# A decoder trunk's second norm: spreading the token factors through DRAM instead of with a diagonal product

## The chip, the cores and the metric

The kernel runs on one core of one Trainium2 chip. The metric is the device time of one execution in microseconds (us). The engines are named as the profile names them: PE is TensorE (PEld its weight loads), DVE is VectorE, ACT is ScalarE, POOL is GpSimd and SP is SyncE, which here only issues the weight transfers.

## The reference

Two layers, each a gated linear recurrence and a sliding-window attention merged, and then a feed-forward block. 256 tokens, width 1024, hidden width 2816, float32. What matters here is the second norm of a layer and what follows it:

```python
def rmsnorm(x, g):
    xf = x.astype(jnp.float32)
    y = xf * lax.rsqrt(jnp.mean(xf * xf, axis=-1, keepdims=True) + EPS)
    return (y * g.astype(jnp.float32)).astype(x.dtype)
...
        x = x + mix @ w_o[l]

        h2 = rmsnorm(x, norm2[l])
        x = x + (jax.nn.silu(h2 @ w_gate[l]) * (h2 @ w_up[l])) @ w_down[l]
```

The norm multiplies each token's row by one factor, the inverse root of its mean square. A factor per token can be applied after the product with a weight matrix as well as before it.

## The kernel before

**Numbers.** Every float32 operand of a large product is cut in a high part, rounded to PE's fast float32 form, and a low part, the rest. ACT casts the high part of a weight (`wh<-raw`), DVE subtracts to get the low one (`wl<-raw,wh`). A product is then three PE products: high by high, high by low, low by high. In the form used for the gate and up products of the feed-forward block, `form_b`, the activations' two parts lie side by side as 512 columns, so that eight wide matmuls (128x512, with `wh`) and eight narrow ones (128x256, with `wl`) make one result of 128 hidden features by 256 tokens. ACT and DVE together drain it from PSUM: ACT copies one half (`COPY zg<-pg`), DVE adds the other (`zg<-pg,zg`); this pair is the function `join`, and DVE's addition is the last that reads the PSUM bank.

**The norm.** The class `Norm` transposes the activations by PE, multiplies by the gain, and cuts them in two parts (`xx`) without the token factors. The factors come out of sums of squares: ACT squares and sums, DVE adds, POOL raises to the power -1/2. That gives `r`, one column of 128 factors (one per partition) for each of the two tiles of 128 tokens. Where a result has tokens on the partitions, `r` is applied as a factor per partition. Where it has tokens along the free axis, as the gate sums do, the 256 factors are needed on all 128 partitions: that is `rb`, and two methods of the class make it. `spread` multiplies the identity by `r` on DVE (`dg`), multiplies a matrix of ones by this diagonal on PE (`rp`, a float32 product) and copies it to `rb` on ACT. `spread_by_row` transposes the two columns on PE to one row in PSUM (`row`), copies it to SBUF on DVE (`flat`), writes it to DRAM by a transfer issued by POOL (L410), and reads it back to all 128 partitions by a second one (L411). The first norm of each layer uses `spread_by_row`, with its result needed some 20 us later; the second norm uses `spread`.

**The feed-forward block.** `layer` works through groups of up to four blocks of 128 hidden features, two blocks at a time in `gate_up`. Such a pair of blocks, called a block below, has two gate sums `pg` and two up sums `pu`. In a layer's first block the order on PE is written out: half of the first `pg`, half of the first `pu`, their second halves (so that the last transposes of the norm fit between), then the call `spread2()`, then the second `pg`, and the second `pu`. After both gate sums are drained to `z`, the function `mid` multiplies `z` by `rb`, takes the sigmoid (`sgm`, on ACT) and multiplies again; the up sums are drained into the same tile `sgm` after that. The up sums get no factor, since that is applied per token after the down product.

**Buffers.** PSUM tiles with the tag `mm` rotate through four banks; a block takes all four (two `pg`, then two `pu`), and the next block the same four in the same order. The prepared weights have five buffers of each kind (`wh`, `wl`), and raw weights three (1 MB each), so weights are prepared up to about four units ahead. One unit is what one `pg` or `pu` needs.

**What sets the order.** PE's instructions stand in the order of the program. For the other engines a scheduler places instructions when the program is built, by its own estimates of when operands are ready; each engine then executes its list strictly in order. A few instructions are pinned with `tc.keep_in_program_order`, among them the two products with the identity and the two transposes of `r`. SP issues the loads of raw weights when a raw buffer has been read for the last time.

Of the kernel before, what the change touches and what calls it, by code (L numbers as in the profile page):

```python
# [44 lines left out]
def trunk(ctx, tc, x, norm1, w_in, lb_logits, hg_norm, attn_sinks, w_pa, w_pb, w_o, norm2,  # L45
# [32 lines left out]
    def psum(name, tag="mm"):  # L78
        return pp.tile([P, 512], F32, tag=tag, name=name, bufs=4 if tag == "mm" else 2)
# [356 lines left out]
    def finish(side):  # L436
        while side[0] is not None:
            step(side)
# [8 lines left out]
    def layer(l, n1):  # L447
# [461 lines left out]
        n2 = Norm(g2[:, l], f"n2_{l}")  # L909
# [21 lines left out]

        for p_ in parts:
            finish(p_)
        rs2, rb2, spread2 = n2.r, n2.wide(), n2.spread
        acc = [[psum(f"acc{l}{t}{c}", "at" if t == 0 else "hg") for c in range(2)] for t in range(NT)]

        def gate_up(gi, b, ah, al):
# [184 lines left out]
    for l in range(DEPTH):  # L1122
        hold = []

        def whole():
            hold.append((yield from layer(l, nx)))

        run(whole())
        nx = hold[0]
# [53 lines left out]
```

## Time and profile before

| | |
|---|---|
| Time, median of 3 runs | 929.61 us (929.11 to 930.15) |
| The profiled execution's own time | 929.29 us |
| Its span, first to last instruction | 927.5 us |
| PE busy | 919.1 us, 99% of the span |
| DVE busy | 675.0 us, 73% |
| ACT busy | 541.2 us, 58% |
| POOL busy | 19.5 us, 2% |
| Moved by DMA | 161.40 MB, 174 GB/s on average |

A row of the order of time reads: start in us, duration in us, engine, line of the program, operation, what is written and read with its shape, a count where neighbours are merged, and in brackets the idle time before it on its engine with what ended it. Almost all computing instructions stand at L59, a helper, so rows are told apart by the names of their tiles. For a matmul the duration contains a tail that overlaps the next one; its real cost is the distance to the next start.

### The profile page before, as it was taken

How to read it: one execution, taken by the hardware profiler on the slowest of the kernel's cores; microseconds unless marked ns; L12 is line 12 of the kernel's file. 1: busy time of each engine (PE TensorE's matmuls, PEld its weight loads, DVE VectorE, ACT ScalarE, POOL GpSimd, SP SyncE). 2: the span in 40 equal slices, each digit the busy share in tenths (PEclk: the TensorE clock that was granted, in tenths of full speed). 3: DMA queues.
4: the chain of work that ended last, by engine and by line, in shares of the span. 5: the costliest groups of instructions: out<-in, count | busy, mean ns of one | idle time of the engine just before them, and what ended most of it. 6: DMA issues, size and time to landing. Idle time of an engine off the chain costs nothing.

```text
span 927.5 us, 14425 instructions
## 1 busy us (share of the span) xinstructions
PE 919.1 (99%) x5716; PEld 780.6 (84%) x5716; DVE 675.0 (73%) x1175; ACT 541.2 (58%) x924; POOL 19.5 (2%) x31
## 2 busy tenths in 40 slices
PE   9999999999999999999999999999999999999997
PEld 7888888888888888888888888888888888888885
DVE  6678899656678766766866787996576787667765
ACT  7567964555456545545555779546463565545553
POOL 2000000001000000000000000000010000000000
PEclk9999999999999999999999999999999999999999
DMA  8725544644546555555555245466445555556641
GB/s 301 262 92 182 163 132 162 213 152 137 182 136 217 192 182 184 190 200 198 167 196 187 94 135 182 140 209 199 137 158 182 177 186 182 183 192 202 194 137 46
DMA packets 111395, 161.40 MB, mean 174 GB/s; under 512 B 2912, under 2 KB 64672, under 8 KB 111328
## 3 DMA queue, kind: packets, MB, share of 16 engines
q1 hardware_dynamic: 110848, 159.42, 52.4%
q8 instruction: 45, 0.74, 0.3%
q10 hardware_dynamic: 320, 0.79, 0.3%
q0 software_dynamic: 160, 0.26, 0.1%
q14 instruction: 22, 0.18, 0.1%
HBM read 159.42 MB, written 1.05 MB: 173 GB/s over the span
## 4 chain that ended last, share of the span: by engine, by line
PE 99%; DVE 0%; ACT 0%; issue 0%; POOL 0%; DVEq 0%; ACTq 0%; POOLq 0%
PE pg L59 13%; PE pu L59 13%; PE acc L59 13%; PE pb L59 10%; PE yb L59 5%; PE v L59 5%; PE gb L59 5%; PE wo L59 5%; PE gate L59 5%; PE ga L59 5%; PE ya L59 5%; PE aq L59 5%; PE akv L59 3%; PE qk L59 1%; PE pv L59 1%; PE o L59 1%
## 5 line engine op out<-in xcount | busy, mean ns | idle before, releaser
L59 DVE TENSOR_TENSOR wl<-raw,wh 128x1024 fp32r<-128x1024 f32 (+1 forms) x301 | 365.4, 1219 | 147.8 <-ACT wh L59 146.8
L59 ACT CAST wh<-raw 128x1024 fp32r<-128x1024 f32 (+1 forms) x301 | 315.1, 1052 | 173.6 <-PE acc L59 45.7
L59 PE MATMUL pu<-xx_n,wh 128*128 128x512 f32 x352 | 92.5, 393 | 0.0
L59 PE MATMUL pg<-xx_n,wh 128*128 128x512 f32 x352 | 92.0, 392 | 0.0
L59 PEld LDWEIGHTS pg<-xx_n,wh 128*128 128x128 f32 x352 | 63.1, 189 | 11.0
L59 PEld LDWEIGHTS pu<-xx_n,wh 128*128 128x128 f32 x352 | 63.0, 189 | 11.0
L59 PE MATMUL acc<-wh,ah 128*128 128x512 f32 x174 | 68.0, 391 | 0.0
L59 PE MATMUL acc<-wh,al 128*128 128x512 f32 x174 | 67.7, 389 | 0.0
L59 PE MATMUL acc<-wl,ah 128*128 128x512 f32 x174 | 67.7, 389 | 0.0
L59 PE MATMUL pb<-xx_n,wh 128*128 128x512 f32 x256 | 65.6, 394 | 0.0
L59 PEld LDWEIGHTS pb<-xx_n,wh 128*128 128x128 f32 x256 | 45.6, 189 | 8.6 <-issue 0.7
L59 PEld LDWEIGHTS pg<-xx_n,wl 128*128 128x128 f32 x352 | 48.4, 190 | 4.1 <-ACT xx_n L59 0.6
L59 PEld LDWEIGHTS pu<-xx_n,wl 128*128 128x128 f32 x352 | 48.4, 190 | 3.6
L59 PE MATMUL pg<-xx_n,wl 128*128 128x256 f32 x352 | 50.3, 284 | 0.0
L59 PE MATMUL pu<-xx_n,wl 128*128 128x256 f32 x352 | 49.7, 282 | 0.0
L59 ACT COPY zg<-pg 128x256 f32<-128x256 f32 x44 | 16.4, 372 | 53.4 <-PE pg L59 53.4
L59 PE MATMUL ga<-wh,xx_n 128*128 128x512 f32 x128 | 41.3, 394 | 0.0
L59 PE MATMUL v<-wh,xx_n 128*128 128x512 f32 x128 | 41.1, 395 | 0.0
L59 PE MATMUL gb<-wh,xx_n 128*128 128x512 f32 x128 | 40.7, 391 | 0.0
L59 PE MATMUL aq<-wh,xx_n 128*128 128x512 f32 x128 | 40.3, 391 | 0.0
L59 PE MATMUL gate<-wh,xx_n 128*128 128x512 f32 x128 | 40.3, 391 | 0.0
L59 PEld LDWEIGHTS acc<-wh,al 128*128 128x128 f32 x174 | 32.7, 188 | 6.8
(265 smaller groups left out, 1660.8 us busy)
## 6 DMA issues: line engine op xcount, KB each, us to landing
raw<-in_w_in SPq DMA_DIRECT2D x58, 1024.0 KB, 5.2
raw<-in_w_gate SPq DMA_DIRECT2D x22, 1024.0 KB, 5.1
raw<-in_w_up SPq DMA_DIRECT2D x22, 1024.0 KB, 5.1
raw<-in_w_down SPq DMA_DIRECT2D x22, 1024.0 KB, 5.0
raw<-in_w_pb SPq DMA_DIRECT2D x8, 1024.0 KB, 5.1
raw<-in_w_pa SPq DMA_DIRECT2D x8, 1024.0 KB, 5.0
raw<-in_w_o SPq DMA_DIRECT2D x8, 1024.0 KB, 5.0
raw<-in_w_in SPq DMA_DIRECT2D x3, 512.0 KB, 7.3
```

The costliest lines, as they stand in the source:

```text
L59: ins = call(*args, **kw)
```

## The change

In `layer`, the second norm's factors are spread by `spread_by_row` instead of `spread`. The call stands at the same place of the program, after the halves of the first gate and the first up sum:

```diff
         for p_ in parts:
             finish(p_)
-        rs2, rb2, spread2 = n2.r, n2.wide(), n2.spread
+        rs2, rb2, spread2 = n2.r, n2.wide(), n2.spread_by_row
         acc = [[psum(f"acc{l}{t}{c}", "at" if t == 0 else "hg") for c in range(2)] for t in range(NT)]
```

The two methods, both there before:

```python
        def spread(self):
            rp = psum(f"rp_{self.name}", "at")
            dg = sm.tile([P, S], F32, tag="dg", name=f"dg_{self.name}", bufs=1)
            for t in range(NT):
                tc.keep_in_program_order(V.tensor_scalar(dg[:, t * P:(t + 1) * P], ident, self.r[t], None, ALU.mult))
            T.matmul(rp[:, :S], ones, dg, start=True, stop=True)
            A.copy(self.rb[:, 0, :], rp[:, :S])

        def spread_by_row(self):
            row = dp.tile([NT, P], F32, tag=f"row_{self.name}", name=f"row_{self.name}")
            flat = sm.tile([1, S], F32, tag="flat", name=f"flat_{self.name}", bufs=1)
            ps = psum(f"row_{self.name}", "at")
            for t in range(NT):
                tc.keep_in_program_order(T.transpose(ps[0:1, t * P:(t + 1) * P], self.r[t], ident))
            V.tensor_copy(flat, ps[0:1, :S])
            nc.gpsimd.dma_start(row.rearrange("t (o p) -> o (t p)", o=1), flat)
            nc.gpsimd.dma_start(self.rb[:, 0, :], row.rearrange("t p -> (t p)").partition_broadcast(P))
```

On PE, in the first block of layer 0 (`pg_2855` is the block's second gate sum, `pu_2856` and `pu_2857` its up sums):

```order
 L59 MATMUL pu_2856<-xx_n_0_2635,wl_2819 128x256 x2
 L59 MATMUL pu_2856<-xx_n_0_2635,wh_2818 128x512 x4
-L59 MATMUL pg_2855<-xx_n_0_2635,wl_2809 128x256 x2
-L59 MATMUL rp_n_0_2894<-dg_n_0_2895,ones 128x256
-L59 MATMUL pg_2855<-xx_n_0_2635,wl_2809 128x256 x6
+L59 MATMUL row_n_0_2896<-ident,r_n_00_2638 1x128
+L59 MATMUL row_n_0_2896<-ident,r_n_01_2639 1x128
+L59 MATMUL pg_2855<-xx_n_0_2635,wl_2809 128x256 x8
 L59 MATMUL pg_2855<-xx_n_0_2635,wh_2808 128x512 x4
 L59 MATMUL pu_2857<-xx_n_0_2635,wh_2830 128x512 x4
```

The ones-by-diagonal product is gone from among the narrow matmuls, and the two transposes stand ahead of them. All else on PE keeps its order.

The same place on DVE before, from the first gate sum's drain to the drains of the first block's two up sums:

```order
L59 TENSOR_TENSOR zg_2858<-pg_2854,zg_2858 128x256
L59 TENSOR_SCALAR dg_n_0_2895<-ident,r_n_00_2638 128x128
L59 TENSOR_SCALAR dg_n_0_2895<-ident,r_n_01_2639 128x128
L59 TENSOR_TENSOR wl_2930<-raw_2806,wh_2929 128x1024
L59 TENSOR_TENSOR wl_2952<-raw_2828,wh_2951 128x1024
L59 TENSOR_TENSOR zg_2858<-pg_2855,zg_2858 128x256
L59 TENSOR_TENSOR zg_2858<-zg_2858,rb_n_0_2636 128x512
L59 TENSOR_TENSOR wl_2958<-raw_2828,wh_2957 128x1024
L59 TENSOR_TENSOR zg_2858<-zg_2858,sgm_2859 128x512
L59 TENSOR_TENSOR wl_2989<-raw_2927,wh_2988 128x1024
L59 TENSOR_TENSOR sgm_2859<-pu_2856,sgm_2859 128x256
L59 TENSOR_TENSOR sgm_2859<-pu_2857,sgm_2859 128x256
```

And now, from the weight split ahead of the copy on (`pg_2966` and `pg_2967` are the second block's gate sums, which were `pg_2964` and `pg_2965` before; weights made after this place have numbers higher by two):

```order
L59 TENSOR_TENSOR wl_2932<-raw_2806,wh_2931 128x1024
L59 COPY flat_n_0_2895<-row_n_0_2896 1x256
L59 TENSOR_TENSOR wl_2954<-raw_2828,wh_2953 128x1024
L59 TENSOR_TENSOR zg_2858<-pg_2855,zg_2858 128x256
L59 TENSOR_TENSOR wl_2960<-raw_2828,wh_2959 128x1024
L59 TENSOR_TENSOR wl_2991<-raw_2929,wh_2990 128x1024
L59 TENSOR_TENSOR zg_2858<-zg_2858,rb_n_0_2636 128x512
L59 TENSOR_TENSOR wl_3015<-raw_2929,wh_3014 128x1024
L59 TENSOR_TENSOR zg_2858<-zg_2858,sgm_2859 128x512
L59 TENSOR_TENSOR zg_2970<-pg_2966,zg_2970 128x256
L59 TENSOR_TENSOR zg_2970<-pg_2967,zg_2970 128x256
L59 TENSOR_TENSOR sgm_2859<-pu_2856,sgm_2859 128x256
```

The products with the identity are gone. The copy to `flat` stands behind one weight split; the product with `rb` stands two splits later than before; and the drains of the second block's gate sums, which stood behind those of the first block's up sums, now stand ahead of them.

On ACT, the rows from the drain of the first block's second gate sum on, now:

```order
L59 COPY zg_2858<-pg_2855 128x256
L59 CAST wh_2959<-raw_2828 128x1024
L59 CAST wh_2990<-raw_2929 128x1024
L59 CAST wh_3014<-raw_2929 128x1024
L59 ACTIVATE sgm_2859<-zg_2858 128x512
L59 COPY zg_2970<-pg_2966 128x256
L59 COPY zg_2970<-pg_2967 128x256
L59 COPY sgm_2859<-pu_2856 128x256
L59 COPY sgm_2859<-pu_2857 128x256
```

Before, the copy of `rp` to `rb` stood at their head, the sigmoid directly behind the first of these casts, and the copies of the up sums ahead of those of the second block's gate sums. From the end of the second block on the lists of all engines are the same again. POOL has two more transfers per layer, after the powers that make `r`. Layer 1 changes in the same way.

## The prediction

> **What bounds the kernel now.** I read the page first, then PE's waits, then the order of time around the two places of the change.
>
> ```profile
> span 927.5 us, 14425 instructions
> PE 919.1 (99%) x5716; PEld 780.6 (84%) x5716; DVE 675.0 (73%) x1175; ACT 541.2 (58%) x924; POOL 19.5 (2%) x31
> ...
> PEclk9999999999999999999999999999999999999999
> ...
> PE 99%; DVE 0%; ACT 0%; issue 0%; POOL 0%; DVEq 0%; ACTq 0%; POOLq 0%
> ```
>
> The chain that ended last is PE alone. The view of PE's waits has a single row:
>
> ```profile
> PE warm L59 <- POOL ident L59: 1.6, 1, 1.6
> ```
>
> So after its start PE never waits for another engine, and its granted clock stays full. What PE no longer executes shortens the run; any wait put in front of a PE instruction lengthens it, because no later PE gap exists that could absorb it. Idle time of DVE (73% busy) and ACT (58%) costs nothing until PE needs something from them.
>
> **The change part by part: PE's own work.** Removed per layer: the product of the ones matrix with the diagonal matrix, at this place (in order of time, layer 0):
>
> ```profile
> 286.75 0.40 PE L59 MATMUL pg<-xx_n,wl 128*128 128x256 f32 x2
> 287.07 0.70 PE L59 MATMUL rp_n<-dg_n,ones 128*128 128x256 f32 x2
> 287.42 1.06 PE L59 MATMUL pg<-xx_n,wl 128*128 128x256 f32 x6
> 288.32 1.09 PE L59 MATMUL pg<-xx_n,wh 128*128 128x512 f32 x4
> 290.16 1.12 PE L59 MATMUL pu<-xx_n,wl 128*128 128x256 f32 x8
> 291.11 1.09 PE L59 MATMUL pu<-xx_n,wh 128*128 128x512 f32 x4
> ```
>
> Eight narrow matmuls alone take 291.11 - 290.16 = 0.95 us; eight with the product among them take 288.32 - 286.75 = 1.57. The product costs 0.62. Added: two transposes of a 128x1 column, which the first norm already has:
>
> ```profile
> 27.15 0.39 PE L59 MATMUL aq<-wl,xx_n 128*128 128x512 f32 x1
> 27.38 0.40 PE L59 MATMUL aq<-wh,xx_n 128*128 128x512 f32 x1
> ...
> 28.05 0.38 PE L59 MATMUL row_n<-ident,r_n 128*1 128x128 f32 x2
> 28.19 0.48 PE L59 MATMUL aq<-wh,xx_n 128*128 128x512 f32 x1
> ...
> 28.50 0.39 PE L59 MATMUL aq<-wl,xx_n 128*128 128x512 f32 x1
> ```
>
> From the first transpose to the second aq after it are 0.45 us, of which one aq takes 0.23 (27.15 to 27.38): the pair costs 0.22. PE gains 0.62 - 0.22 = 0.40 per layer, and from there runs 0.4 ahead of the old times. DVE's two products with ident and ACT's copy of rp go too; they are off the path and worth nothing by themselves.
>
> **The new chain: when the row has come back.** DVE's copy to flat now stands behind a weight split, not at the place of the diagonal. The two executions of the same chain in the first norm price the rest; the second block of rows is of layer 1, and the last two are the broadcast's landing in each:
>
> ```profile
> 28.47 0.41 DVE L59 COPY flat_n<-row_n 1x256 f32<-1x256 f32 x1 [0.34 <-PE row_n L59]
> 29.18 0.71 POOL L410 DMA_DIRECT2D row_n<-flat_n  x1 [10.01 <-DVE flat_n L59]
> 31.98 0.57 POOL L411 DMA_DIRECT2D rb_n<-row_n  x1 [2.08 <-DMA row_n<-flat_n]
> ...
> 485.55 0.41 DVE L59 COPY flat_n<-row_n 1x256 f32<-1x256 f32 x1 [1.07 <-PE row_n L59]
> 486.25 0.57 POOL L410 DMA_DIRECT2D row_n<-flat_n  x1 [17.02 <-DVE flat_n L59]
> 488.44 0.56 POOL L411 DMA_DIRECT2D rb_n<-row_n  x1 [1.62 <-ACT aq L59]
> ...
> DMA to landing us min/median/max: 3.5/3.5/3.5
> ...
> DMA to landing us min/median/max: 4.3/4.3/4.3
> ```
>
> From the end of the copy to the first issue pass 0.30 and 0.29 us, between the issues 2.80 and 2.19, from the second issue to its landing 3.5 and 4.3: 6.6 and 6.8 in all. On POOL nothing else is queued then. Now the engines around the old place:
>
> ```profile
> 286.06 2.00 ACT L59 CAST wh<-raw 128x1024 fp32r<-128x1024 f32 x2
> 287.15 2.36 DVE L59 TENSOR_TENSOR wl<-raw,wh 128x1024 fp32r<-128x1024 f32 x2
> 290.31 0.69 DVE L59 TENSOR_TENSOR zg<-zg,rb_n 128x512 f32<-128x512 f32 x1
> 290.92 1.22 DVE L59 TENSOR_TENSOR wl<-raw,wh 128x1024 fp32r<-128x1024 f32 x1
> 292.29 1.05 ACT L59 CAST wh<-raw 128x1024 fp32r<-128x1024 f32 x1 [0.61 <-PE pu L59]
> 293.91 2.00 PE L59 MATMUL pg<-xx_n,wh 128*128 128x512 f32 x8
> 294.51 0.75 DVE L59 TENSOR_TENSOR sgm<-pu,sgm 128x256 f32<-128x256 f32 x2
> 295.04 0.37 ACT L59 COPY zg<-pg 128x256 f32<-128x256 f32 x1 [1.16 <-PE pg L59]
> 295.30 1.06 ACT L59 CAST wh<-raw 128x1024 fp32r<-128x1024 f32 x1
> 297.63 1.07 PE L59 MATMUL pu<-xx_n,wh 128*128 128x512 f32 x4
> 297.83 0.37 ACT L59 COPY zg<-pg 128x256 f32<-128x256 f32 x1 [0.95 <-PE pg L59]
> ```
>
> The split that now precedes the copy still waits for its cast (ACT, from 286.06), so it starts at 287.15 and leaves DVE at about 288.3 (of two splits in 2.36 us, the second starts 2.36 - 1.22 = 1.14 after the first). Copy 288.3 to 288.7, plus 6.6 to 6.8: the broadcast lands at 295.3 to 295.5. I add 0.2 for the wake of DVE (an estimate: in the first norm POOL issued 0.30 after the landing of its own row) and take **T = 295.6** for the product of zg with rb, which in the old run started at 290.31.
>
> **What is queued behind it.** By the new order DVE then executes, strictly one after the other: zg by rb, one weight split, zg by its sigmoid, two drains of the second block's gate sums (pg), and only then the drains of the first block's up sums (pu). In the old order the pu drains came at 294.51. Pitches from the rows: zg by rb 0.61 (290.31 to 290.92), the split 1.14, zg by sigmoid 0.61 (the same shape), the pg drains 0.33 each (two drains take 0.75, one 0.42), the pu drain 0.42: 3.44 us. The first pu bank is drained at 295.6 + 3.44 = 299.04. ACT's copies ahead of the drains fit between: the sigmoid ends near 297.0, the copies of both pg by 297.9 (the second follows the end of its PE product, 297.83 - 0.4), and that of pu follows zg by sigmoid.
>
> Who waits? The pool for these sums has four banks. Block one holds pg, pg, pu, pu; the second block's two pg take the first two, and its first pu has to take a pu bank. PE reaches this matmul at 297.63 - 0.40 = 297.23 and has to wait until about 299.1. **Stall 1.9 us per layer**, against the 0.4 gained: 1.5 net.
>
> Behind the stall nothing else is late: the splits of the next four weight units stand ahead of the drains, a unit lasts PE 2.8 us (eight wide matmuls at 0.23, eight narrow in 0.95), and the first split behind the drains is for a product that PE reaches four units, some 11 us, after the stall. Weight loads on SP hang on splits that stand ahead of zg by rb, or are needed far later; no cost. Both layers are alike: the old rows stand 456.9 us apart,
>
> ```profile
> L59 ACT COPY rb_n<-rp_n x2: 373/373/373, 288.0 to 744.9; 128x256 f32<-128x256 f32 x2
> ```
>
> so the sum is 2 x (1.9 - 0.4) = **+3.0 us**. The profiled execution took 929.29 us (span 927.5 and 1.8 around it): 932.3. The median of the runs is 929.61, 0.3 more, so it gives 932.6; I say 932.5.
>
> **Bounds.** Below: however early the row lands, the split behind zg by rb needs a cast of ACT which needs the weight buffer of the second block's first product. That product ended just ahead of 295.04, now 294.64; plus 1.06 the cast is ready at 295.7, and split to pu drain are 1.14 + 0.61 + 0.66 + 0.42 = 2.83: 298.5. The stall has a floor of 1.3, net 0.9 per layer, 931.4 in all. Above: a landing 1.4 us later (somewhat under twice the 0.8 between 3.5 and 4.3) makes T = 297.0, a stall of 3.3, net 2.9, 935.4.
>
> The Trainium skill ("DMA: Bandwidth & Descriptors", Anatomy of one DMA, the gpsimd path) gives each such transfer a fixed cost of about 2.0 us plus bytes over 436 GB/s, thus an estimate of 2.0 and 2.3 for the two; by that T would be near 293.6, the floor would hold, and the time would be 931.4. This trace's second transfer disagrees with 3.5 and 4.3, and I go by the trace.
>
> **The rivals.**
>
> *Hidden.* The drains come in time and only PE's 0.4 per layer is left: 929.6 - 0.8 = 928.8. For it: the old pu drains ended at 295.3, 2.4 us before PE needed the bank, and PE had no wait. It decides if DVE drains the first pu by 297.2, hence T at 293.8 or earlier and the cast of 295.30 off DVE's way. Against it: the measured chain gives 295.6, and the cast alone gives 298.5.
>
> *The row comes late.* The raw weight loads share the DMA engines with the broadcast; with a load on them at full rate the landing may exceed 4.3. Each further microsecond is one per layer; at T = 297 the time is 935.4. For it: 3.5 and 4.3 already differ by 0.8 for the same bytes. Against it: both were taken amid the same loads.
>
> *The clock drops too.* PE without work may lose speed when it restarts. The run's start bears on it:
>
> ```profile
> 6.48 0.79 PE L59 MATMUL akv<-wl,xx_n 128*128 128x512 f32 x1
> ...
> 8.99 0.39 PE L59 MATMUL akv<-wl,xx_n 128*128 128x512 f32 x1
> ```
>
> The same matmul took 0.79 us about 5 us after PE's first work and 0.39 later, half speed for 5 us or so, though the clock row shows full. If a stall set PE back to that, 5 us at half speed lose 2.5 per layer: 932.6 + 5.0 = 937.6 from the forecast, 940 with the late row. For it: PE would be idle for 1.9 to 3.3 us. Against it: at the start PE had done nothing at all, and here 1.9 us of idleness is preceded by 280 us of work. The Trainium skill ("TensorE: Matmul & The Clock Gate", Why this matters for your kernels) warns of gaps of more than about 3 us, after which the clock falls to half. By that the forecast's stall stays under it, and only the late row's reaches it; no wait of this trace shows which.
>
> **How the numbers follow.** Forecast, stall of 1.3 to 2.6 per layer: 0.67. Hidden: 0.10. Late row at full clock: 0.12. Clock drop: 0.11. The predicted time is the forecast's. 80% range: from 930.4, which leaves most of the hidden case out, to 936.0, which takes in the late row and leaves out most of the clock's. This kernel's measurement tells about 0.2% (1.9 us) from no change. Faster by more needs 1.9 us, more than the 1.24 of removed product work: 0.03. Within: nearly all of the hidden case and the forecast's floor, which lies just on the border: 0.17. Slower: 0.80.
>
> **What would show it.** In the new profile PE's waits get a row of pu waiting for DVE's sgm, twice, 1.9 us each; the rb product starts some 5 us later than before, near 295.6 and 752.5; DVE has an idle row released by the DMA of rb; the first pu of the second block starts near 299.1; part 2 keeps PEclk at 9. The row pair should cost PE 0.22. If PE has no new wait, the drain argument is wrong. If PE waits but the rb product starts near 294, the chain's price is wrong and ACT's cast is the floor. If the matmuls after the stall take twice their time, the clock case holds.

## The result, and the profile after

The changed kernel takes **937.95 us** (median of 4 runs, 936.77 to 938.92) against 929.88 for the kernel before on the same chip. The ratio is 1.0087 (95% interval 1.0075 to 1.0099): 8 us slower, where +3 was forecast, and above the range's upper end of 936.0. The profiled execution of the changed kernel took 938.92 us.

The page of the changed kernel, its span, PE's busy time, the clock in 40 slices and the engines of the chain that ended last:

```profile
span 936.9 us, 14440 instructions
...
PE 922.3 (98%) x5716; PEld 782.7 (84%) x5716; DVE 674.0 (72%) x1173; ACT 541.6 (58%) x922; POOL 21.8 (2%) x35
...
PEclk9999999999999999999999999999999989999999
...
PE 96%; DMA 2%; DVE 1%; issue 1%; ACT 0%; POOL 0%; DVEq 0%; ACTq 0%; POOLq 0%
```

The chain is no longer PE alone: DMA and DVE have 3% of it. PE is busy for 3.2 us more than before although it has less to do, and in one slice its clock isn't full. The view of PE's waits:

```profile
PE pu L59 <- DVE zg L59: 6.2, 2, 3.2
```

One new wait in each layer, 6.2 us in both together. Here is layer 0 in order of time:

```profile
287.33 0.38 PE L59 MATMUL row_n<-ident,r_n 128*1 128x128 f32 x2
...
288.50 1.09 PE L59 MATMUL pg<-xx_n,wh 128*128 128x512 f32 x4
288.87 0.40 DVE L59 COPY flat_n<-row_n 1x256 f32<-1x256 f32 x1
288.98 0.37 SPq L190 DMA_DIRECT2D raw<-in_w_up  x1
...
289.56 0.57 POOL L410 DMA_DIRECT2D row_n<-flat_n  x1 [5.15 <-DVE flat_n L59]
...
294.78 0.56 POOL L411 DMA_DIRECT2D rb_n<-row_n  x1 [4.65 <-DMA row_n<-flat_n]
...
298.17 0.69 DVE L59 TENSOR_TENSOR zg<-zg,rb_n 128x512 f32<-128x512 f32 x1 [3.40 <-DMA rb_n<-row_n]
...
300.52 0.75 DVE L59 TENSOR_TENSOR zg<-pg,zg 128x256 f32<-128x256 f32 x2
...
300.99 1.21 PE L59 MATMUL pu<-xx_n,wh 128*128 128x512 f32 x4 [3.01 <-DVE zg L59]
...
301.18 0.75 DVE L59 TENSOR_TENSOR sgm<-pu,sgm 128x256 f32<-128x256 f32 x2
...
302.04 1.11 PE L59 MATMUL pu<-xx_n,wl 128*128 128x256 f32 x8
```

Between the two POOL issues lie 5.22 us. The view of the DMA issues between 284 and 300 us has the KB of each and the us from issue to landing:

```profile
raw<-in_w_up SPq DMA_DIRECT2D x1, 1024.0 KB, 5.1
...
rb_n<-row_n POOLq DMA_DIRECT2D x1, 128.0 KB, 3.3
row_n<-flat_n POOLq DMA_DIRECT2D x1, 1.0 KB, 4.7
```

The 1 KB of the row needed 4.7 us. Then the broadcast takes 3.4 until DVE goes on, and 2.82 later PE has its bank: 3.01 us of waiting. (This execution is 0.58 us late here already, from its start; PE's row that began at 285.83 before begins at 286.41.) In layer 1 the same happens, and something more:

```profile
758.25 0.69 DVE L59 TENSOR_TENSOR zg<-zg,rb_n 128x512 f32<-128x512 f32 x1 [3.57 <-DMA rb_n<-row_n]
...
761.07 2.07 PE L59 MATMUL pu<-xx_n,wh 128*128 128x512 f32 x4 [3.19 <-DVE zg L59]
...
762.95 1.91 PE L59 MATMUL pu<-xx_n,wl 128*128 128x256 f32 x8
```

The four wide matmuls take 2.07 us where layer 0 has 1.21, the eight narrow ones 1.91 where it has 1.11. The stretches of time around it give the cause, the granted clock, third number from the end of each row:

```profile
758.00:760.00 2.00, 0.00 (x0) 0.00 (x0) 1.75 (x3) 1.02 (x3) 0.00 (x0) 1.00 0.00 0
760.00:761.00 1.00, 0.00 (x0) 0.00 (x0) 1.00 (x4) 0.43 (x3) 0.00 (x0) 0.67 0.00 0
761.00:763.00 2.00, 1.93 (x5) 1.54 (x6) 2.00 (x6) 1.67 (x4) 0.00 (x0) 0.50 0.75 215
763.00:765.00 2.00, 2.00 (x10) 1.98 (x9) 2.00 (x4) 0.86 (x2) 0.00 (x0) 0.50 0.87 310
...
767.00:769.00 2.00, 2.00 (x13) 1.79 (x13) 1.32 (x2) 0.92 (x2) 0.00 (x0) 0.96 0.00 0
```

From the wait's last part to shortly after 767 PE runs at half speed (the row left out has 0.50 too), which costs 6 x 0.5 + 2 x 0.04 = 3.1 us. In layer 0 the clock stays full after a wait of almost the same length.

The account of this execution goes against the profiled one of before, whose span is 9.4 us shorter (927.5). At the two waits PE's next product starts 3.18 and 3.36 us later than it would have: from start to start are 4.11 us (296.88 to 300.99) and 4.29 (756.78 to 761.07), where before the same distance is 0.93 (296.70 to 297.63). The view's 3.01 and 3.19 are shorter because they begin behind the tail of the product ahead. So: delays at the waits +6.5, removed work -0.8, clock +3.1, lateness from the start +0.6, together 9.4.

### The profile page after: what moved, and what is told of

Its sections match the earlier page's. It is cut to its first block, busy times and chain, and to the rows that moved or that the text cites. A ratio compares the mean times of both kernels' runs of the same rounds, so it can differ in the third digit from the quotient of the medians.

```text
span 936.9 us, 14440 instructions
## 1 busy us (share of the span) xinstructions
PE 922.3 (98%) x5716; PEld 782.7 (84%) x5716; DVE 674.0 (72%) x1173; ACT 541.6 (58%) x922; POOL 21.8 (2%) x35
## 3 DMA queue, kind: packets, MB, share of 16 engines
HBM read 159.68 MB, written 1.05 MB: 172 GB/s over the span
## 4 chain that ended last, share of the span: by engine, by line
PE 96%; DMA 2%; DVE 1%; issue 1%; ACT 0%; POOL 0%; DVEq 0%; ACTq 0%; POOLq 0%
PE pu L59 13%; PE acc L59 13%; PE pg L59 12%; PE pb L59 10%; PE yb L59 5%; PE v L59 5%; PE wo L59 5%; PE gb L59 5%; PE gate L59 5%; PE ga L59 5%; PE ya L59 5%; PE aq L59 5%; PE akv L59 3%; PE qk L59 1%; PE pv L59 1%; PE o L59 1%
## 5 line engine op out<-in xcount | busy, mean ns | idle before, releaser
L59 PE MATMUL pu<-xx_n,wh 128*128 128x512 f32 x352 | 94.9, 400 | 6.2 <-DVE zg L59 6.2
```

Of the source, the lines that this page charges most:

```text
L59: ins = call(*args, **kw)
```

## The experiments

The theory after the result: the 1 KB write to DRAM takes nearly 5 us because a weight load of 1 MB is issued 0.6 us ahead of it; the row then reaches DVE late; DVE holds drains behind the product that needs the row; PE waits for a drain; and the wait can halve its clock. Each step got runs of its own.

**The drains.** In this kernel the drains of the first block's up sums stand in the program ahead of the work on `rb`, and the sigmoid goes to a tile of its own. The row stays as late as it was.

```diff
+            gat = ztile([P, 2, S], f"gat{l}", "hx") if first else sgm
             def mid():
                 V.tensor_tensor(z, z, rb2, ALU.mult)
-                A.activation(sgm, z, AF.Sigmoid)
-                V.tensor_tensor(z, z, sgm, ALU.mult)
+                A.activation(gat, z, AF.Sigmoid)
+                V.tensor_tensor(z, z, gat, ALU.mult)
...
-                mid()
                 join(sgm[:, 0], pu[0])
...
                 join(sgm[:, 1], pu[1])
                 used()
                 used()
+                mid()
```

> The changed kernel, with the first block's two up sums drained into their tile before the gate sums meet rb (the sigmoid gets a tile of its own for that block, or it would be overwritten). The row's way through DRAM is as in the changed kernel. Theory (PE is stopped by the up sums' banks alone, since their drains stand behind the product with rb on DVE): rb still comes near 298.2 us in layer 0, DVE still waits for it about 3 us, but PE has no wait, the granted clock is 0.999 and the time is 929.9 - 2 x 0.4 = 929.1. Rival (PE hangs on something else that is late with rb, for instance weight splits or the gate sums' banks): PE still waits more than 1 us per layer and the time stays above 932.

Measured: 929.12 us, ratio 0.9993 (0.9984 to 1.0002). In order of time, at the same place:

```profile
297.67 1.07 PE L59 MATMUL pu<-xx_n,wh 128*128 128x512 f32 x4
298.04 0.69 DVE L59 TENSOR_TENSOR zg<-zg,rb_n 128x512 f32<-128x512 f32 x1 [3.18 <-DMA rb_n<-row_n]
...
298.65 0.42 DVE L59 TENSOR_TENSOR zg<-pg,zg 128x256 f32<-128x256 f32 x1
```

DVE still waits for the row, until 298.04, but PE begins its up sum at 297.67 with no wait. The late row costs nothing once no drain that PE needs is queued behind it.

Is it the new order alone that saves time? The kernel before, with its diagonal product, got the same edit:

> The kernel before, with its product with the diagonal matrix, but with the drains of the first block's up sums ahead of the work on rb, as in e1. Theory (this order is worth nothing where PE has no wait): 929.6 to 930.0, the same as before. Rival (the order itself saves something, and e1's 0.7 us comes from it): 929.1 to 929.3.

Measured: 929.36 us, ratio 0.9999 (0.9991 to 1.0008). The order is worth nothing where nothing is late.

**The place of the transfers.** Here the row is made ahead of the second half of the up sum, so that its write leaves before the weight load.

```diff
-                for ks in (range(KT // 2), range(KT // 2, KT)):
-                    yield from form_b(pg[0], n2, units[0], ks)
-                    yield from form_b(pu[0], n2, units[2], ks)
+                yield from form_b(pg[0], n2, units[0], range(KT // 2))
+                yield from form_b(pu[0], n2, units[2], range(KT // 2))
+                yield from form_b(pg[0], n2, units[0], range(KT // 2, KT))
+                spread2()
+                yield from form_b(pu[0], n2, units[2], range(KT // 2, KT))
                 join(z[:, 0], pg[0])
-                spread2()
```

> The changed kernel, with the spread called one step earlier (behind the second half of the first gate sum, ahead of the second half of the first up sum), so that the copy and the row's write go out near 287.3 us instead of 289.6, ahead of the weight load that is issued at 289.0. Theory (the write took 4.7 us because it shared the DMA engines with that load): from the issue of the write to that of the broadcast 2.2 to 2.8 us as in the first norm; rb lands between 293 and 294.5 (the broadcast may now share with the load); the drains come in time or at most 0.5 us late, and the time is 929 to 930.5. Rival (a write at this place takes about 5 us by itself, for example because DVE keeps POOL's descriptors back): broadcast issued at 292.3, rb at 295.6 to 296, a wait of 1 to 1.5 us per layer and 931 to 932.

Measured: 929.28 us, ratio 0.9994 (0.9984 to 1.0003).

```profile
287.63 0.57 POOL L410 DMA_DIRECT2D row_n<-flat_n  x1 [2.89 <-DVE flat_n L59]
...
289.31 0.37 SPq L190 DMA_DIRECT2D raw<-in_w_up  x1
...
289.80 0.56 POOL L411 DMA_DIRECT2D rb_n<-row_n  x1 [1.60 <-DMA row_n<-flat_n]
...
294.75 0.69 DVE L59 TENSOR_TENSOR zg<-zg,rb_n 128x512 f32<-128x512 f32 x1 [2.20 <-DMA rb_n<-row_n]
```

These rows are layer 0's: the write now lands in 1.6 us, and it is the broadcast, 0.5 behind the load, that takes 4.9. In layer 1 the write needs 3.1 with no load ahead of it, for a reason that stays open, and the broadcast 4.4. PE keeps one wait of 0.3 us. This run moves the row earlier by 1.4 us as well, so it doesn't isolate the load.

Both cures together:

> Both cures at once: the row is made and written ahead of the second half of the up sums, and the drains of the up sums stand ahead of the work on rb. Theory: no PE wait, 929.8 less the 0.4 us that PE saves in each layer, 929.0 (928.8 to 929.3); faster than e1 and e3 by no more than 0.3. Rival (the PE saving is not there, 929.12 and 929.28 came from something else): 929.6 or more.

Measured: 928.81 us against 929.4, ratio 0.9992 (0.9983 to 1.0002). It has the lowest median of all, and PE's saving of 0.8 us would fit the interval, but so would no change: it can't be told from the kernel before.

**The load.** To isolate it, the two weight loads at this place in each layer were cut to an eighth; the kernel leaves out the rest of these weights. Nothing else moves: PE's, DVE's and ACT's instructions keep their order.

```diff
+        thin = j in (47, 48, 122, 123)
-        for a, b in {0: ((0, 1), (1, 2), (2, 4)), 1: ((0, 2), (2, 4))}.get(j, ((0, nk),)):
+        for a, b in ((0, 1),) if thin else {0: ((0, 1), (1, 2), (2, 4)), 1: ((0, 2), (2, 4))}.get(j, ((0, nk),)):
...
-            parts = [raw[:, :, i * P:(i + 1) * P] for i in range(n // P)]
+            parts = [raw[:, 0:1, i * P:(i + 1) * P].to_broadcast([P, nk, P]) if thin else
+                     raw[:, :, i * P:(i + 1) * P] for i in range(n // P)]
```

> Leaves out: the two weight loads issued around the second norm's row transfers in each layer (w_up at 288.98 and w_gate at 292.24 in layer 0, and the same two in layer 1) fetch one eighth of their data, 128 KB, and the splits read that eighth for all of the tile; the instructions of PE, DVE and ACT and their order are those of the changed kernel. Theory (the loads are what makes the write to DRAM slow): from the issue of the write to that of the broadcast 2.2 to 3.0 us in place of 5.2, broadcast as before 3.3 to 3.5, product of zg with rb near 295.2 to 296.2 in place of 298.2, PE waits 0.3 to 1.0 in each layer, no half-speed stretch, granted clock .998 or more, 930.0 to 931.5 us. Rival (the write is slow in this place for a cause of its own): 5.2 us between the issues, waits of 3 us, 936 to 938 us.

Measured: 930.45 us, ratio 1.0012 (1.0003 to 1.0021). In order of time (the two issues stand at L412 and L413 here):

```profile
288.41 0.35 SPq L191 DMA_DIRECT2D raw<-in_w_up  x1
...
289.00 0.57 POOL L412 DMA_DIRECT2D row_n<-flat_n  x1 [5.16 <-DVE flat_n L59]
...
291.17 0.56 POOL L413 DMA_DIRECT2D rb_n<-row_n  x1 [1.60 <-DMA row_n<-flat_n]
...
294.54 0.69 DVE L59 TENSOR_TENSOR zg<-zg,rb_n 128x512 f32<-128x512 f32 x1 [0.32 <-DMA rb_n<-row_n]
294.71 1.05 ACT L59 CAST wh<-raw 128x1024 fp32r<-128x1024 f32 x1 [1.76 <-PE pg L59]
...
295.80 1.23 DVE L59 TENSOR_TENSOR wl<-raw,wh 128x1024 fp32r<-128x1024 f32 x1 [0.57 <-ACT wh L59]
...
298.01 1.20 PE L59 MATMUL pu<-xx_n,wh 128*128 128x512 f32 x4 [0.60 <-DVE zg L59]
```

Same queue, same place, a load of 128 KB in place of 1 MB: 2.17 us between the issues, not 5.22. PE waits 0.6 in each layer, and what sets that is no longer the row but ACT's cast of 294.71, for which DVE's split waits until 295.80. So the loads are the cause of the late write. Both were thinned, the one ahead of the write and the one 2.7 us behind it; that it is the first which counts is read from the landings below, not from this run alone.

**Another queue.** The row's write issued by ACT's queue, in a copy of the method that only the second norm uses:

```diff
-            nc.gpsimd.dma_start(row.rearrange("t (o p) -> o (t p)", o=1), flat)
+            nc.scalar.dma_start(row.rearrange("t (o p) -> o (t p)", o=1), flat)
```

> The changed kernel, with the row's write to DRAM issued by ACT instead of POOL at the same place (the broadcast stays with POOL). Theory (the load occupies the DMA engines that both use): the write still takes 4 to 5 us, and the time stays at 935 to 939. Rival (it is POOL's way of issuing that is slow here): the write takes about 2 us, rb lands near 295.5, the wait shrinks to 1 to 2 us, and the time is 931 to 933.

Measured: 937.05 us, ratio 1.0078 (1.0063 to 1.0093).

```profile
288.73 0.47 ACTq L420 DMA_DIRECT2D row_n<-flat_n  x1
...
291.72 0.60 POOL L421 DMA_DIRECT2D rb_n<-row_n  x1 [7.88 <-DMA row_n<-flat_n]
...
297.28 0.69 DVE L59 TENSOR_TENSOR zg<-zg,rb_n 128x512 f32<-128x512 f32 x1 [3.08 <-DMA rb_n<-row_n]
...
300.10 1.19 PE L59 MATMUL pu<-xx_n,wh 128*128 128x512 f32 x4 [2.69 <-DVE zg L59]
```

The time is the theory's, the transfers are not. From the write's issue to the broadcast's are 2.99 us, 2.2 less, as the rival had it; then the broadcast takes 5.5 in place of 3.3 in layer 0, 5.0 in layer 1, and PE waits 2.69 and 2.35. Both waits were followed by half speed (301.42 to 304.83 and 762.22 to 765.63), so the shorter waits saved hardly any time. Why the write got through here, with the same load ahead of it, is open: it left by another queue, but also nearer to the load, 0.32 us behind its issue and not 0.58.

**PE's clock.** If idleness halves the clock, useless work in the wait should keep it. Nine, then fourteen products of the ones matrix with the identity (in two passes each, 18 and 28 rows) went in front of the matmul that waits, into a bank that nothing reads:

```diff
+                if gi == 0:
+                    hot = psum(f"hot{l}", "at")
+                    for i in range(9):
+                        T.matmul(hot[:, (i % 4) * P:(i % 4 + 1) * P], ones, ident, start=True, stop=True)
                 for i in range(2):
                     yield from form_b(pu[i], n2, units[2 + i])
```

> The changed kernel, with nine small products of constants (ones by identity, into a bank that nobody reads) on PE ahead of the matmul that waits, in the first group of each layer. They fill about 2.8 us of the 3.2 us wait (an estimate from 0.62 us for the twice as wide product of ones and diagonal) and compute nothing that is used. Theory (the stall costs 2.9 net per layer, and what is above that is the clock, which falls because PE stands still): the granted clock stays at 0.999 in every run, no half-speed stretch, time 929.9 + 5.8 = 935.7, and the runs agree within 0.5. Rival (the slow stretch is not caused by the idle time, or the wait itself is longer than in the profile): clock 0.993 to 0.996 and 937 to 939 as the changed kernel.

Measured: 936.58 us (934.80 to 939.69), ratio 1.0076 (1.0054 to 1.0098). Inconclusive: the 18 rows took only 2.17 us, and the broadcast of layer 0 needed 4.6 here, so PE still waited 2.38 there and was at half speed for 3.4 us; in layer 1 it waited 0.88 and kept its clock. With 14 products:

> The changed kernel with 28 products of the ones matrix with the identity (written to a bank that nothing reads) in front of the first matmul that waits, some 3.4 us in each layer by the 2.17 us that 18 of them took. Theory (PE's idleness is what halves its clock): PE is idle for 0.5 us or less in each place, no stretch at half speed, granted clock .998 or more in every run, 935.0 to 936.3 us, all runs within 1 us. Rival (the clock falls for another cause, or a wait of any length does it): clock .995 to .996 in some runs and 937 to 939 us.

Measured: 935.34 us in 4 runs between 934.69 and 935.94, ratio 1.0063 (1.0049 to 1.0076).

```profile
297.22 3.29 PE L59 MATMUL hot<-ident,ones 128*128 128x128 f32 x28
297.36 0.69 DVE L59 TENSOR_TENSOR zg<-zg,rb_n 128x512 f32<-128x512 f32 x1 [3.18 <-DMA rb_n<-row_n]
...
300.26 1.17 PE L59 MATMUL pu<-xx_n,wh 128*128 128x512 f32 x4
```

PE's up sum starts 3.04 us behind the first useless product in both layers (297.22 to 300.26 here), nearly the delays of 3.18 and 3.36 without them, but PE isn't idle, and the clock is full through the run: its idleness is what halved it. The useless products fill the whole wait, so the delay is theirs as much as the row's. By the rows it costs 2 x (3.04 - 0.40) = 5.3 us, by the medians 5.9. Of the changed kernel's 8.1 us the other 2.2 are then the clock, less some 0.5 by which PE is held up for longer there.

**When the clock drops.** Waits of 3.01 and 3.19 us had opposite results, and those of 2.35 to 2.69 cost the clock, so length is not all. In the kernel before, PE was stopped on purpose: in five blocks of each layer a chain of small copies on DVE holds up the first up sum.

```diff
+                k = 5 * l + ngap[l]
+                if (2 * gi + b) % 2 == 1 and ngap[l] < 5:
+                    ngap[l] += 1
+                    tick = sm.tile([P, 64], F32, tag="tick", name=f"tick{k}", bufs=1)
+                    V.tensor_copy(tick, z[:, 1, :64])
+                    for _ in range([0, 2, 4, 6, 8, 10, 13, 16, 20, 26][k]):
+                        V.tensor_copy(tick, tick)
+                    T.matmul(pu[0][:, :64], ones, tick, start=True, stop=True)
```

> The kernel before, with PE stopped on purpose at ten places: in five blocks of each layer a chain of small DVE copies (0, 2, 4, 6, 8 in layer 0, 10, 13, 16, 20, 26 in layer 1) starts when the second gate sum has been drained, and a small product in front of the first up sum waits for its end. The gaps rise from about 1.5 us to about 5. Theory (idleness alone halves the clock, but whether it does depends on when the idle stretch falls): after gaps under 2 us no half speed, after gaps over 4 us always, from 2 to 4 us in some; half-speed stretches of 3.4 or 7 us. Rival (a fixed length decides): one length splits the ten places, all above lose the clock and none below. Second rival (idleness has nothing to do with it, the drop in the changed kernel came from elsewhere): the clock stays full at all ten.

> As the run with rising gaps, with the lengths in falling order (26, 20, 16, 13, 10 copies in layer 0, 8, 6, 4, 2, 0 in layer 1). Theory: the same lengths, between 2 and 4 us, now and then give another answer than in the other run. First rival: each length gives the same answer in both. Second rival: full clock throughout.

Measured, in one execution each: 953.01 and 955.71 us. The waits were not what was meant, since PE had other work at most of the places: in the first run 3.70, 6.00, 1.82 and six of 0.7 or less, in the second 9.66, 5.54 and six of 0.7 or less. All five long ones were followed by half speed, the 1.82 too, which the theory of that moment had put below the border; none of the short ones was. But the beginnings and ends of half speed, worked out from the clock in stretches of 1 or 2 us, showed a rule. In the first run they are 302.54 to 305.96, 766.76 to 773.58 and 910.12 to 913.52; from the first to the second beginning are 464.22 us, 136.0 times 3.413, and to the third 178.0 times. In the second run 302.00 to 312.24 and 776.46 to 779.88: 139.0 times. That was put to a test with other lengths (0, 25, 27, 29, 31 copies in layer 0 and 1, 24, 26, 28, 33 in layer 1):

> The kernel before, with PE stopped on purpose at ten places as in the runs with rising and falling gaps, but with 24 to 33 copies at the places where PE has other work first, so that more of the waits lie between 1 and 4 us. Theory (worked out from five traces: PE's idleness is looked at in stretches of 3.41 us that follow one another on one grid through the whole run; a stretch in which PE is idle for more than about 1.8 us, 52%, is followed by half speed, and half speed ends behind a stretch in which it is idle for less than about 0.5): all beginnings and ends of half speed in this run lie a whole number of 3.413 us apart, within 0.1; a wait under 1.7 us is never followed by half speed; a wait of 1.8 to 3.5 us is, where one stretch of that grid holds 1.8 us or more of it, and is not where the grid's line cuts it into two shorter pieces. Rival (the length of the wait alone decides, at about 1.8 us, and the 3.01 us of the changed kernel's first layer was an exception): all waits from 1.8 us on are followed by half speed, beginning at no common grid.

Measured, in one execution: 977.73 us. Two of its waits, and the clock behind the second:

```profile
820.52 0.41 PE L59 MATMUL pu<-tick,ones 128*128 128x64 f32 x2 [1.36 <-DVE tick L59]
...
856.05 0.41 PE L59 MATMUL pu<-tick,ones 128*128 128x64 f32 x2 [1.82 <-DVE tick L59]
```

```profile
856.00:857.00 1.00, 0.95 (x5) 0.84 (x6) 1.00 (x1) 0.00 (x0) 0.00 (x0) 0.79 0.97 307
857.00:859.00 2.00, 2.00 (x9) 1.80 (x8) 0.03 (x1) 0.00 (x0) 0.00 (x0) 0.50 0.98 346
859.00:860.00 1.00, 1.00 (x6) 0.90 (x6) 0.00 (x0) 0.00 (x0) 0.00 (x0) 0.50 0.01 3
860.00:861.00 1.00, 1.00 (x6) 0.82 (x5) 0.00 (x0) 0.11 (x1) 0.00 (x0) 1.00 0.00 0
```

Half speed begins at 857 - 2 x (1 - 0.79) = 856.58 and ends at 860.00, 3.42 later. All ten waits, with the beginning and end of the half speed that followed:

| Wait, us | from, to | half speed | beginnings less 303.62, in units of 3.413 us |
|---|---|---|---|
| 3.70 | 298.66, 302.36 | 303.62 to 307.04 | 0 |
| 1.58 | 337.61, 339.19 | none | |
| 2.05 | 372.89, 374.94 | 375.30 to 378.72 | 21.00 |
| 3.51 | 410.19, 413.70 | 412.84 to 419.68 | 32.00 |
| 3.97 | 450.12, 454.09 | 453.80 to 457.22 | 44.00 |
| 3.93 | 779.99, 783.92 | 784.90 to 788.32 | 141.01 |
| 1.36 | 819.16, 820.52 | none | |
| 1.82 | 854.23, 856.05 | 856.58 to 860.00 | 162.01 |
| 2.27 | 891.29, 893.56 | 894.12 to 897.54 | 173.01 |
| 4.43 | 928.79, 933.22 | 931.68 to 938.50 | 184.01 |

One grid of 3.413 us carries all eight, over 630 us of the run. In each case the stretch of the grid ahead of the beginning holds at least 1.82 us of PE's idleness, and half speed ends behind the first stretch with 0.4 us of it or less (after 3.51 the next stretch still holds 0.86, after 4.43 1.54, and both last for two). The lower side of that border is one case of the falling run: 1.76 us of its wait of 5.54 fell in the first stretch, and half speed began only behind the next one, which was idle throughout. Put on the changed kernel, whose half speed begins at 760.34: the wait of layer 1 (757.88 to 761.07) has 2.46 us in one stretch; that of layer 0 (297.98 to 300.99) is cut by a line of the grid at 299.54 into 1.56 and 1.45, and nothing happens. No wait of the last run happened to be cut so, and this one case is all that speaks against the rival that 1.8 us of a wait suffice wherever they fall; the grid itself is shown.

## Why the prediction was wrong, step by step

- **PE's own work: right.** The pair of transposes and eight narrow matmuls take 288.50 - 287.33 = 1.17 us, so the pair costs 0.22 as forecast. Whether the gain of 0.8 shows in the time isn't settled: 929.12 and 928.81 without waits point to it, but the intervals include no change.
- **The flat copy and the first issue: right.** The copy at 288.3 and the issue at 289.0 are the rows at 288.87 and 289.56 less the 0.58 of the late start.
- **The first transfer: this is the step that failed.** "Between the issues 2.80 and 2.19" came from the first norm and was carried to the second, where it measured 5.22 and 5.40. The prediction's sentence that both were taken amid the same loads did not hold. These stretches of the kernel before, around the first norm's writes (issued at 29.18 and 486.25), and those of the changed kernel around the second norm's, have the share of the DMA engines and GB/s as last two numbers:

```profile
29.00:30.00 1.00, 1.00 (x6) 0.82 (x5) 1.00 (x1) 0.35 (x1) 0.71 (x1) 1.00 1.08 385
30.00:31.00 1.00, 1.00 (x6) 0.84 (x5) 0.12 (x1) 0.45 (x1) 0.00 (x0) 1.00 0.87 301
31.00:32.00 1.00, 1.00 (x6) 0.81 (x5) 0.00 (x0) 1.00 (x3) 0.02 (x1) 1.00 0.52 120
...
487.00:488.00 1.00, 1.00 (x6) 0.84 (x5) 0.19 (x1) 0.39 (x1) 0.00 (x0) 1.00 0.02 1
```

```profile
291.00:292.50 1.50, 1.50 (x10) 1.28 (x10) 1.21 (x1) 0.03 (x1) 0.00 (x0) 1.00 1.03 361
292.50:294.00 1.50, 1.50 (x12) 1.38 (x11) 0.45 (x1) 1.02 (x1) 0.00 (x0) 1.00 1.04 285
```

  In the first norm of layer 0 the load ahead of the write had been issued 3.0 us earlier, at 26.22, and landed at 31.5 (5.3); the write landed at 31.7 (2.5). In layer 1 the load ahead was just ending (it landed at 487.1), and the write took 1.6. In the second norm the load ahead was issued only 0.6 us earlier, at 288.98, and landed at 294.1 (5.1); the write landed at 294.3 (4.7), and in layer 1 at 754.4 behind a load that landed at 754.2. So wherever the load ahead lasted for longer than those 1.6 us, the write that POOL issued landed 0.2 us behind that load; the same holds in both layers of the runs with the drains first and with useless work. The price of 2.80 was the rest of a load, and here nearly a whole one was left. The rows for this stood in the trace of before: its loads at the second norm, and those around the first. The range's upper end took 1.4 us on the landing as a bound; the write alone brought 2.4 to 3.2. With the loads thinned it took 2.17, the lower of the two prices.
- **The second transfer: right in size.** 3.3 in both layers, against 3.5 and 4.3, with a weight load beside it that had been issued 2.5 us ahead. T came out at 298.17 - 0.58 = 297.6, not 295.6.
- **What PE waits for: a step too late.** The prediction had PE wait for the drain of the first block's up sum. But PE starts at 300.99, when the first of the two drains of the second block's gate sums (from 300.52, 0.41 each) has just ended, and before the up sum's drain begins at 301.18. By these times the bank of the new up sum is the one that this drain set free; that banks follow in a fixed order, as told above of the kernel before, doesn't hold across the two orders. From T to PE's start pass 2.82 us, the same in both layers and in the run with ACT's queue, not 3.44. With T = 295.6 the stall would have been 1.2, not 1.9. This error of 0.6 hid a part of the other, of 2.0. Of the 5.1 us between the forecast's +3.0 and the measured +8.1 the longer waits are 2.7 (3.18 + 3.36 in place of 2 x 1.9); the rest, 2.4, is put down to the clock, for which the run with useless work gives 1.7 to 2.2.
- **The floor: right in kind.** With the loads thinned ACT's cast sets the wait, as the floor had it. By the distance of the starts the delay is 0.76 us (296.32 to 298.01, less 0.93); the floor's 1.3, less the error of 0.6 that it shares, would be 0.7. Measured so, the sum is 2 x (0.76 - 0.40) = +0.7 us; the runs gave +1.05, with an interval from 0.3 to 2.0.
- **The rivals.** "Row late" had the mechanism, and 935.4 as its time; with the clock kept by useless work it was 935.34. That they agree so closely is luck in part: T was 297.6 and not 297.0, and 2.82 us passed behind it and not 3.44, and the two errors cancel. "Clock drops too" came true on top of it. Its 2.5 us per layer at half speed were 3.1 in one layer and nothing in the other. Its chance of 0.11 rested on a stall of 1.9 being too short, and the runs put the border lower than the prediction did: an idle time of 1.82 was enough, twice. A stall of 1.9, counted as there from start to start, is an idle time of 1.7 (3.18 against 3.01 above), just short of that. But the forecast's stall went up to 2.6, an idle time of 2.4, and by the grid that leaves at least 1.8 in one stretch of 3.41 in about two thirds of all positions ((3.41 - 2.4 + 2 x 0.6) / 3.41 = 0.65, an estimate from these rows). Even with its own T the forecast should have given the clock more weight. The Trainium skill ("TensorE: Matmul & The Clock Gate", Part 1) tells of a free-running window of 3.4 us, which is the grid seen here, and lets the clock fall after at least one idle window; the seven waits of 1.82 to 2.69 us that cost the clock here disagree, and just over half a window sufficed.

## What to carry to other kernels

Price a small transfer at the place where it will be issued, not where the same code already stands: look up which loads leave within a microsecond or two ahead of it, since 1 KB that POOL issued behind a load of 1 MB landed with the 1 MB. If an operand may be late, look at what an engine that works in order has queued behind its use, and put what others wait for, here the drains, ahead; that alone took away the 8 us here. And treat each wait of a busy PE of about 1.8 us or more as a wait and a possible 3.4 us or more at half speed, half of which is lost.

## What was not expected of the hardware

- The clock drops on a grid of 3.413 us that runs through the whole execution; a wait's position on it decides as much as its length (3.01 us without, 1.82 with a drop).
- A write of 1 KB issued by POOL took 1.6 us in quiet and 4.5 to 4.9 when it was issued 0.6 us behind a load of 1 MB on another queue (eight cases in four runs): it landed 0.2 us behind that load.
- A broadcast of 128 KB took 3.2 to 3.3 with the loads thinned, and mostly as long beside a load issued 2.5 us earlier (4.6 once); 4.9 when issued 0.5 behind a load, and 5.0 and 5.5 within 0.2 of one. From the write's issue to the broadcast's landing are 5.5 us with the loads thinned, 7.1 (layer 0) with the row made early, 8.5 and 8.7 in the changed kernel, 8.5 and 8.1 with ACT's queue: to speed up the one transfer put the other beside a load.
